# A blockwise triangular inversion that makes one column a step, with an earlier gate and a fifth key buffer

## The chip, the cores and the metric

The program runs on one core of one Trainium2 chip. The metric is the device time of one execution in microseconds (us). Five engines take part, each with its own queue of instructions in order: TensorE (PE; PEld is its weight load), VectorE (DVE), ScalarE (ACT), GpSimd (POOL) and SyncE (SP), which issues the DMAs.

## The reference

A decoder trunk of two layers on a sequence of 1024 with width 1024. Layer 0 mixes by a gated delta rule (GDN) with 8 heads of 128, layer 1 by stick-breaking attention; each is followed by a SwiGLU feed-forward network and a gated embedding. The change touches the GDN alone (and, through the planner's prices, the order elsewhere). Per head and chunk the reference solves a unit lower triangular system:

```python
kk = jnp.einsum('bnhrd,bnhsd->bnhrs', k, k)
a_low = jnp.where(strict, beta[..., None] * kk * decay_mat, 0.0)
rhs = jnp.concatenate([v * beta[..., None], k * (beta * jnp.exp(G))[..., None]], axis=-1)
sol = lax.linalg.triangular_solve(a_low + eye, rhs, left_side=True, lower=True, unit_diagonal=True)
# then, chunk by chunk:
v_new = u_c - jnp.einsum('bhcd,bhde->bhce', w_c, state)
o = jnp.einsum('bhcd,bhde->bhce', q_c, state) + jnp.einsum('bhrs,bhse->bhre', qk_c, v_new)
state = state * gl_c[..., None, None] + jnp.einsum('bhcd,bhce->bhde', k_c, v_new)
```

## The kernel before

The kernel works with chunks of 128 and with sixteen units u = 2h + half (head h, half of the sequence; four chunks each). Projections and the feed-forward network are matmuls of 512 columns, each value split in a high and a low part, so that one product is three matmuls. The small products of the GDN (128 x 128) are in float32 and show as two records each, transposes as one.

**The order is written by a planner at build time.** Every piece of work is a Python generator; `Flow.run` (line 228) steps a simulated clock, which is PE's, and always lets the ready generator of lowest key run; when none is ready it takes the next dense matmul (`gdn_dense`, line 780) as filler. `Flow.cost` (line 114) prices each instruction; on DVE it is 0.069 us plus elements/960. The order in which instructions are emitted is the order of each engine's queue on the chip, so a wrong price doesn't change the result, but puts a PE instruction ahead of its operand.

**GDN.** Dense order (`gdn_order`, line 868): for each head h the keys k of head h+1 (both halves), gates g of h, then q and v of h+1. `gdn_features` (line 885) filters each projection (three DVE steps on `ca`) and puts it through Silu on ACT. `gdn_inv(h)` (line 948) waits at line 954, loads the decay rows (`Gb`: DMA, a mask on POOL, Exp on ACT), transposes the keys into `kt`, makes the triangle `LT`, and takes its four 32 x 32 diagonal blocks through DRAM (`Ld`) into `Ls`, with one partition per eighth part of a block. There the inverse of all blocks of a head is built in `xr` by 31 steps of two DVE instructions each, with `yr` between them (lines 1028 to 1032). The result goes back by DRAM (`Xd`) into `X0`, three rounds of 128 x 128 products join the blocks (`Z`), and the recurrence `gdn_rec(u)` (line 1111) uses it: per chunk a chain PE `rc`, DVE `vin`, PE `r`, DVE `vE`, PE `rc`, DVE `Sm`. `gdn_prep(u)` (line 1069) marks ("p", u) after its `rq`; `cdone` counts finished recurrences. Inversion and recurrence have the same key, ahead of all else. The attention of layer 1 uses two POOL masks per diagonal block (`select`, line 1918).

The loop of the inversion, before:

```python
for t in range(B - 1, 0, -1):
    y = self.g("yr", (P, CG, B))
    nc.vector.tensor_tensor(y[:, :, :t], x[:, :, t : t + 1].to_broadcast([P, CG, t]), Lv[:, :t, t].unsqueeze(1).to_broadcast([P, CG, t]), op=ALU.mult)
    yield
    nc.vector.tensor_tensor(x[:, :, :t], x[:, :, :t], y[:, :, :t], op=ALU.subtract)
```

Of the kernel before, what the change touches and what calls it, by code (L numbers as in the profile page):

```python
# [8 lines left out]
F32 = mybir.dt.float32  # L9
F32R = mybir.dt.float32r  # L10
AF = mybir.ActivationFunctionType
ALU = mybir.AluOpType
# [3 lines left out]
P = 128  # L16
# [3 lines left out]
H = 8  # L20
HW = 512
NC = S // P
# [9 lines left out]
B = 32  # L32
NB = P // B
CG = 8
# [3 lines left out]
def const_table():  # L38

    i = np.arange(P)  # L40
    r, c = i[:, None], i[None, :]
    tab = [b.astype(np.float32) for b in (r == c, r <= c, r >= 0 * c, r >= c, r < c)]
    tab.append(-(r // B > c // B).astype(np.float32))
    g = i[:, None, None] % (B // CG)
    e = np.arange(B)[None, None, :] == CG * g + np.arange(CG)[None, :, None]
    tab += list(e.reshape(P, 2, P).astype(np.float32).transpose(1, 0, 2))
    return np.ascontiguousarray(np.stack(tab, 1))
# [35 lines left out]
class Flow:  # L83
# [29 lines left out]

    def cost(self, eng, op, out, ins, kw):
        n = 1
        for d in out.shape[1:]:
            n *= d
        psum = any(x.space == PSUM for x in ins)
        if eng == "pe":
            if op != "transpose" and ins[0].dtype == F32R:  # L120
                return max(n, P) / 2400.0 + 0.0127
            return max(n, P) * (2 if op == "transpose" else 4) / 2400.0 + (0.003 if op == "transpose" else 0.0107)
        if eng == "dve":
            if op == "memset":
                return 0.06 + n / 3840.0
            tail = 0.06 if any(x.shape[-1] == 1 for x in ins) and n > 1 else 0.0
            fast = op in ("tensor_copy", "tensor_scalar") and not psum
            return 0.069 + tail + n / (1920.0 if fast else 960.0)
        if eng == "act":
            us = (0.052 if psum else 0.094) + n / 1200.0  # L130
            return us + 0.093 * (len(ins) - 1) + (0.235 if "accum_out" in kw else 0.0)
        if op == "tensor_tensor":
            return 0.295 + 0.166 * n if kw.get("op") == ALU.pow else 0.148 + n * 0.002104
        return 0.12 + n / 1085.0

    def shared(self, eng, op, outs, ins, kw, t, c):

# [132 lines left out]
class Net:  # L270
# [366 lines left out]
        flow.mark(("pp", layer))  # L637


    BUFS = {"kf": 5, "qf": 4, "vf": 2, "sg": 2, "Gb": 4, "eGb": 1, "kt": 4, "LT": 2, "vt": 3, "QK": 3, "zz": 2, "Z": 3, "ou": 2, "xe": 2, "ca": 2, "Ls": 1, "xr": 1, "rq": 3, "sc": 2, "yr": 1, "vin": 1}  # L640

    def g(self, tag, shape=(P, HW), dt=F32):
        return self.t(self.gs, tag, shape, dt, bufs=self.BUFS.get(tag, 2))
# [76 lines left out]
    def gdn_gates(self, abs_):  # L720

        nc, gc, ad = self.nc, self.gc, self.ad
        NJ = H * NC
        pt = yield from self.bank()
        ptv = pt[:, : NC * 16].rearrange("p (c j) -> p c j", j=16)
        for c in range(NC):
            nc.tensor.transpose(ptv[:, c], abs_[c // 4][:, (c % 4) * P : (c % 4 + 1) * P], self.ident[:16, :16])
        yield
        t = gc.tile([P, NC, 16], F32, name="abt")
        nc.vector.tensor_copy(t, ptv)  # L730
        self.unbank(pt)
        x = gc.tile([P, H, NC], F32, name="xg")
        tv = t.rearrange("p c j -> p j c")
        nc.vector.tensor_tensor(x, tv[:, :H], ad[:, 1].unsqueeze(2).to_broadcast([P, H, NC]), op=ALU.add)
        yield
        e = gc.tile([P, H, NC], F32, name="eg0")
        nc.scalar.activation(e, x, AF.Abs)
        nc.scalar.activation(e, e, AF.Exp, scale=-1.0)
        ea = gc.tile([P, H], F32, name="ea")
        nc.scalar.activation(ea, ad[:, 0], AF.Exp)  # L740
        nc.scalar.activation(e, e, AF.Ln, bias=1.0)
        yield
        nc.vector.scalar_tensor_tensor(e, x, 0.0, e, op0=ALU.max, op1=ALU.add)
        g = gc.tile([P, H, NC], F32, name="g")
        nc.vector.scalar_tensor_tensor(g, e, -1.0, ea.unsqueeze(2).to_broadcast([P, H, NC]), op0=ALU.mult, op1=ALU.mult)
        yield
        gf = g.rearrange("p h c -> p (h c)")
        pr = yield from self.bank()
        self.mmul(pr[:NJ, :P], gf, self.cst[:, C_TRI])
        yield  # L750
        rows = gc.tile([NJ, 2, P], F32, name="rows")
        nc.vector.tensor_copy(rows[:, 0], pr[:NJ, :P])
        self.unbank(pr)
        yield
        nc.sync.dma_start(self.gD[0], rows[:, 0])
        self.flow.mark("rows")
        nc.scalar.activation(rows[:, 1], rows[:, 0], AF.Exp)
        pG = yield from self.bank()
        self.mmul(pG[:, :NJ], self.cst[:, C_TRI], gf)
        self.mmul(pG[:, NJ : 2 * NJ], self.ones, gf)  # L760
        yield
        nc.sync.dma_start(self.gD[1], rows[:, 1])
        GG = gc.tile([P, 3, NJ], F32, name="GG")
        nc.vector.tensor_copy(GG[:, :2].rearrange("p a j -> p (a j)"), pG[:, : 2 * NJ])
        self.unbank(pG)
        self.neG = gc.tile([P, NJ], F32, name="neG")
        self.nG = gc.tile([P, NJ], F32, name="nG")
        nc.vector.tensor_scalar(self.nG, GG[:, 0], -1.0, None, op0=ALU.mult)
        nc.vector.tensor_tensor(GG[:, 2], GG[:, 1], GG[:, 0], op=ALU.subtract)
        yield  # L770
        EE = gc.tile([P, 3, NJ], F32, name="EE")
        nc.scalar.activation(EE, GG, AF.Exp)
        self.beta = gc.tile([P, H, NC], F32, name="beta")
        nc.scalar.activation(self.beta, tv[:, H:], AF.Sigmoid)
        self.eG, self.gl, self.E = EE[:, 0], EE[:, 1], EE[:, 2]
        yield
        nc.vector.tensor_scalar(self.neG, self.eG, -1.0, None, op0=ALU.mult)
        self.flow.mark("gates")
# [106 lines left out]
    def gdn_features(self, n, u, ps):  # L885

        nc = self.nc
        h, hf = u // 2, u % 2
        yield
        if n == "g":  # L890
            f = self.g("sg")
            nc.scalar.activation(f, ps, AF.Silu)
            self.give("mm")
            self.st[u]["g"] = f
            self.flow.mark(("g", u))
            return
        yield from self.take("xe")
        yield from self.take("ca")
        xe = self.g("xe", (P, HW + 3))
        nc.scalar.copy(xe[:, 3:], ps)  # L900
        self.give("mm")
        if hf == 0:
            nc.gpsimd.memset(xe[:, :3], 0.0)
        else:
            nc.vector.tensor_copy(xe[:, :3], self.conv_tail[n])
        yield
        if hf == 0:
            self.conv_tail[n] = self.g("cy" + n, (P, 3))
            nc.vector.tensor_copy(self.conv_tail[n], xe[:, HW:])
        ca = self.tmp()  # L910
        tl = "qkv".index(n) * H + h
        nc.scalar.activation(ca, xe[:, :HW], AF.Copy, scale=self.conv[:, 0, tl : tl + 1])
        yield
        for j in range(1, 4):
            nc.vector.scalar_tensor_tensor(ca, xe[:, j : j + HW], self.conv[:, j, tl : tl + 1], ca, op0=ALU.mult, op1=ALU.add)
            yield
        f = self.g(n + "f")
        nc.scalar.activation(f, ca, AF.Silu)
        self.give("xe", "ca")
        self.st[u][n] = f  # L920
        self.flow.mark((n, u))
# [26 lines left out]
    def gdn_inv(self, h):  # L948

        nc, flow = self.nc, self.flow  # L950
        us = (2 * h, 2 * h + 1)
        chunks = [slice(c * P, (c + 1) * P) for c in range(4)]
        j0 = us[0] * 4
        yield lambda: flow.done("rows") and self.cdone >= us[0] - 2 and (h == 0 or ("p", us[0] - 1) in flow.at) and (h < 2 or ("w", us[0] - 3) in flow.at)
        Gb = [self.g("Gb") for _ in us]

        def decay():
# [16 lines left out]
        for i, u in enumerate(us):  # L974
# [3 lines left out]
            kt = self.g("kt")  # L978
# [12 lines left out]
        yield lambda: flow.done("gates")  # L991
        bt = self.beta.rearrange("p h c -> p (h c)")[:, j0 : j0 + 8]
        nc.vector.tensor_tensor(rkb, rk, bt, op=ALU.mult)
        nc.vector.tensor_tensor(brk2, rkb, rk, op=ALU.mult)
        yield lambda: flow.done(("D", h))
        LT = self.g("LT", (P, 2, HW))
        for i, u in enumerate(us):
# [23 lines left out]
        Ls = self.g("Ls", (P, B * B))  # L1021
        src = Ld.rearrange("c b s r -> (c b) (s r)").unsqueeze(1).to_broadcast([8 * NB, B // CG, B * B])
        nc.sync.dma_start(Ls, src)
        x = self.g("xr", (P, CG, B))
        nc.scalar.copy(x, self.masks[:, 1:].rearrange("p a (j s) -> p (a j) s", s=B))
        yield
        Lv = Ls.rearrange("p (s r) -> p s r", r=B)
        for t in range(B - 1, 0, -1):
            y = self.g("yr", (P, CG, B))
            nc.vector.tensor_tensor(y[:, :, :t], x[:, :, t : t + 1].to_broadcast([P, CG, t]), Lv[:, :t, t].unsqueeze(1).to_broadcast([P, CG, t]), op=ALU.mult)  # L1030
            yield
            nc.vector.tensor_tensor(x[:, :, :t], x[:, :, :t], y[:, :, :t], op=ALU.subtract)
            yield
        flow.mark(("x", h))
        nc.sync.dma_start(Xd.rearrange("c b r k -> (c b r k)").rearrange("(p n) -> p n", p=P), x.rearrange("p j s -> p (j s)"))
# [1087 lines left out]
```

## Time and profile before

| what | value |
|---|---|
| median of 3 runs | 2801.99 us (2799.51 to 2804.23) |
| the profiled execution | 2799.09 us |
| its span, first to last instruction | 2797.3 us |
| mean granted TensorE clock | 0.997 |
| busy: PE, PEld, DVE, ACT, POOL | 98%, 81%, 70%, 47%, 31% |

The GDN fills the first 660 us of the span or so, the attention about 1500 to 1950. A PE that is busy is not a PE at its peak, because a matmul's record is longer than the time until the next one starts; so the number of matmuls in a stretch says more than the busy share. All instructions bear line 64 (a helper that records them); they are told apart by their tiles. In the rows, `tp<-cst,kf` reads "into tile tp, from cst and kf".

### The profile page before, as it was taken

The page shows a single profiled execution, that of the slowest core. Times are in us where ns is not written, and L with a number is a line of the kernel's source. Part 1 is how long each engine was busy: PE and PEld are TensorE (multiplying, and loading weights), DVE is VectorE, ACT ScalarE, POOL GpSimd, SP SyncE. Part 2 cuts the span into 40 slices and gives each one's busy share as a digit, 9 for nine tenths or more (in the row PEclk, how much of TensorE's full clock was granted, in tenths as well). Part 3 has the DMA queues.
Part 4 walks back from the last instruction along what each step waited for, and adds up shares of the span by engine and source line. Part 5 has one row for each costly group of instructions (what it writes and reads, how often), then busy time and mean ns, then how long its engine had stood idle before and what let it go on. Part 6 is the DMA issues. An engine that isn't in the chain of part 4 may idle for free.

```text
span 2797.3 us, 37777 instructions
## 1 busy us (share of the span) xinstructions
PE 2750.1 (98%) x13203; PEld 2271.7 (81%) x13203; DVE 1969.8 (70%) x3733; ACT 1326.0 (47%) x2694; POOL 870.4 (31%) x742
## 2 busy tenths in 40 slices
PE   9999999999999999999999999999999999999999
PEld 7888888878878888888878888887878888888777
DVE  7778877884776565477867778787696565557783
ACT  6655555543443343322335778787543433322241
POOL 0111111100166666443201222221036766734400
PEclk9999999999999999999999999999999999999999
DMA  4412222237524444587333111114524444477622
GB/s 146 143 58 81 67 74 74 74 111 252 178 91 158 154 147 147 211 314 307 138 132 102 50 53 57 54 57 153 207 70 151 145 154 148 157 287 283 273 98 105
DMA packets 165631, 395.89 MB, mean 142 GB/s; under 512 B 34048, under 2 KB 35392, under 8 KB 155968
## 3 DMA queue, kind: packets, MB, share of 16 engines
q1 hardware_dynamic: 165440, 393.48, 39.7%
q8 instruction: 104, 1.70, 0.3%
q14 instruction: 87, 0.71, 0.1%
HBM read 274.29 MB, written 119.11 MB: 141 GB/s over the span
## 4 chain that ended last, share of the span: by engine, by line
PE 79%; DVE 12%; ACT 3%; DMA 3%; issue 3%; SPq 1%; POOL 1%; ACTq 0%; DVEq 0%; POOLq 0%
PE dn L64 38%; PE mm L64 29%; PE tp L64 3%; PE z L64 3%; PE c L64 2%; PE o L64 2%; DVE x L64 1%; DVE yr L64 1%; DVE ca L64 1%; DVE xr L64 1%; PE po L64 1%; DVE wlo L64 1%; DVE u L64 1%; DVE v L64 1%; SPq L64 1%
## 5 line engine op out<-in xcount | busy, mean ns | idle before, releaser
L64 PE MATMUL mm<-x,whi 128*128 128x512 f32 x2848 | 941.0, 400 | 8.5 <-DVE x L64 5.4
L64 PEld LDWEIGHTS mm<-x,whi 128*128 128x128 f32 x2848 | 529.6, 189 | 107.9 <-DVE x L64 8.4
L64 PE MATMUL mm<-x,wlo 128*128 128x512 f32 x1424 | 569.3, 400 | 0.0
L64 PE MATMUL dn<-x,whi 128*128 128x512 f32 x1776 | 548.9, 390 | 1.8 <-DVE v L64 0.9
L64 POOL TENSOR_TENSOR wlo<-raw,whi 128x512 fp32r<-128x512 f32 x236 | 345.5, 1485 | 441.1 <-ACT whi L64 414.8
L64 ACT CAST whi<-raw 128x1024 fp32r<-128x1024 f32 x231 | 242.9, 1052 | 447.7 <-DVE raw L64 262.5
L64 PEld LDWEIGHTS dn<-x,whi 128*128 128x128 f32 x1776 | 333.1, 188 | 73.7 <-DVE x L64 2.9
L64 PE MATMUL dn<-x,wlo 128*128 128x512 f32 x888 | 345.7, 389 | 0.0
L64 PEld LDWEIGHTS mm<-x,wlo 128*128 128x128 f32 x1424 | 269.0, 189 | 46.1 <-issue 0.2
L64 PE MATMUL dn<-hx,whi 128*128 128x512 f32 x864 | 266.5, 389 | 0.3 <-DVE hx L64 0.2
L64 DVE TENSOR_TENSOR tt<-u,tt 128x512 fp32r<-128x512 f32 x140 | 143.6, 1026 | 81.8 <-ACT tt L64 81.7
L64 PEld LDWEIGHTS dn<-x,wlo 128*128 128x128 f32 x888 | 166.7, 188 | 34.4
L64 PEld LDWEIGHTS dn<-hx,whi 128*128 128x128 f32 x864 | 162.1, 188 | 34.9 <-DVE hx L64 0.9
L64 DVE TENSOR_TENSOR v<-v,dn 128x512 f32<-128x512 f32 x112 | 76.6, 685 | 156.3 <-PE dn L64 155.8
L64 DVE TENSOR_TENSOR wlo<-raw,whi 128x512 fp32r<-128x512 f32 x226 | 154.4, 696 | 29.4 <-ACT whi L64 29.1
L64 PE MATMUL dn<-hx,wlo 128*128 128x512 f32 x432 | 168.5, 390 | 3.4 <-POOL wlo L64 3.4
L64 POOL TENSOR_TENSOR wlo<-sw,whi 128x512 fp32r<-128x512 f32 x102 | 144.3, 1432 | 2.0 <-ACT whi L64 2.0
L64 ACT CAST tt<-u 128x512 fp32r<-128x512 f32 x140 | 84.9, 620 | 123.7 <-DMA yD<-tt 100.3
L64 DVE TENSOR_TENSOR E<-E,dn 128x512 f32<-128x512 f32 x132 | 90.0, 684 | 69.9 <-PE dn L64 67.7
L64 DVE SCALAR_TENSOR_TENSOR ca<-xe,conv,ca 128x512 f32<-128x512 f32 x144 | 108.4, 754 | 8.9 <-ACT ca L64 8.5
L64 POOL TENSOR_TENSOR rs<-ms,nhalf 128x4 f32<-128x4 f32 x11 | 12.4, 1123 | 328.9 <-DVE ms L64 328.9
L64 PE MATMUL dn<-y,whi 128*128 128x512 f32 x352 | 108.3, 389 | 0.0
(379 smaller groups left out, 5159.5 us busy)
## 6 DMA issues: line engine op xcount, KB each, us to landing
yD<-tt SPq DMA_DIRECT2D x296, 256.0 KB, 2.2
x<-yD SPq DMA_DIRECT2D x58, 1024.0 KB, 11.7
raw<-f_s SPq DMA_DIRECT2D x84, 512.0 KB, 3.6
raw<-d_s SPq DMA_DIRECT2D x40, 512.0 KB, 4.0
raw<-w_in SPq DMA_DIRECT2D x33, 512.0 KB, 3.6
hx<-yD SPq DMA_DIRECT2D x16, 1024.0 KB, 11.2
x<-oD SPq DMA_DIRECT2D x27, 512.0 KB, 6.7
raw<-g_out SPq DMA_DIRECT2D x16, 512.0 KB, 5.8
```

Of the source, the lines that this page charges most:

```text
L64: r = issue(*args, **kw)
```

## The change

The inverse is built the other way round. Before, step t took column t of the block, multiplied it with column t of the triangle (elements 32 apart in `Ls`) and subtracted the outer product from all columns to its left. After, step s makes column s alone: the columns to its right are multiplied with row s of the triangle (elements side by side), and a `tensor_reduce` sums each row of products into column s. The last columns and the unit entries are put in beforehand by two ACT copies instead of one. The sign moves into `LT` (`brk2` gets a factor of -1), so the mask of the joining step turns positive.

Further: `kt` gets five buffers, `sc` three; the gate at line 954 opens one recurrence earlier; small tiles of `gdn_gates` move into `vt` buffers; the filter's tail is kept per head. The planner's prices change: `tensor_reduce` is priced by its input, a DVE input with stepped elements costs 0.085 us more, a POOL mask 0.4 us plus elements/1400.

```diff
-    tab.append(-(r // B > c // B).astype(np.float32))
+    tab.append((r // B > c // B).astype(np.float32))
...
-        for d in out.shape[1:]:
+        for d in (ins[0] if op == "tensor_reduce" else out).shape[1:]:
...
+            if any(x.shape[-1] > 1 and x.ap[-1][0] > 1 for x in ins):
+                tail += 0.085
...
-        return 0.12 + n / 1085.0
+        return 0.4 + n / 1400.0 if op == "affine_select" else 0.1 + n / 1085.0
...
-    BUFS = {... "kt": 4, ... "sc": 2, ...}
+    BUFS = {... "kt": 5, ... "sc": 3, ...}
...
-        t = gc.tile([P, NC, 16], F32, name="abt")
+        room = self.g("vt")
+        t = room[:, : NC * 16].rearrange("p (c j) -> p c j", j=16)
...
-        yield lambda: flow.done("rows") and self.cdone >= us[0] - 2 and (h == 0 or ("p", us[0] - 1) in flow.at) and (h < 2 or ("w", us[0] - 3) in flow.at)
+        yield lambda: flow.done("rows") and self.cdone >= us[0] - 3 and (h < 2 or ("p", us[0] - 3) in flow.at) and (h < 2 or ("w", us[0] - 3) in flow.at)
...
-        nc.vector.tensor_tensor(brk2, rkb, rk, op=ALU.mult)
+        nc.vector.scalar_tensor_tensor(brk2, rkb, -1.0, rk, op0=ALU.mult, op1=ALU.mult)
...
         x = self.g("xr", (P, CG, B))
-        nc.scalar.copy(x, self.masks[:, 1:].rearrange("p a (j s) -> p (a j) s", s=B))
+        y = self.g("yr", (P, CG, B))
+        rows = self.masks[:, 1:].rearrange("p a (j s) -> p (a j) s", s=B)
+        nc.scalar.copy(x[:, :, B - 1], rows[:, :, B - 1])
+        nc.scalar.copy(y[:, :, : B - 1], rows[:, :, : B - 1])
         yield
         Lv = Ls.rearrange("p (s r) -> p s r", r=B)
-        for t in range(B - 1, 0, -1):
-            y = self.g("yr", (P, CG, B))
-            nc.vector.tensor_tensor(y[:, :, :t], x[:, :, t : t + 1].to_broadcast([P, CG, t]), Lv[:, :t, t].unsqueeze(1).to_broadcast([P, CG, t]), op=ALU.mult)
-            yield
-            nc.vector.tensor_tensor(x[:, :, :t], x[:, :, :t], y[:, :, :t], op=ALU.subtract)
+        for s in range(B - 2, -1, -1):
+            nc.vector.tensor_tensor(y[:, :, s + 1 :], x[:, :, s + 1 :], Lv[:, s, s + 1 :].unsqueeze(1).to_broadcast([P, CG, B - 1 - s]), op=ALU.mult)
+            yield
+            nc.vector.tensor_reduce(x[:, :, s], y[:, :, s:], axis=mybir.AxisListType.X, op=ALU.add)
             yield
```

## Rows read from the trace of the kernel before

**Rows 1.** The page: its first line, and section 1 (busy time by engine).

```profile
span 2797.3 us, 37777 instructions
PE 2750.1 (98%) x13203; PEld 2271.7 (81%) x13203; DVE 1969.8 (70%) x3733; ACT 1326.0 (47%) x2694; POOL 870.4 (31%) x742
```

**Rows 2.** Windows: length, busy by engine, clock, DMA; feed-forward, then attention.

```profile
1050.00:1100.00 50.00, 50.00 (x222) 41.40 (x221) 29.19 (x39) 18.92 (x27) 32.23 (x23) 1.00 0.47 159
...
1600.00:1650.00 50.00, 50.00 (x251) 41.88 (x250) 40.53 (x85) 40.76 (x97) 9.28 (x18) 1.00 0.14 48
```

**Rows 3.** Chain of waits, one run of 128 x 128 products: start, length, what.

```profile
275.88 2.68 PE tp L64 x24
```

**Rows 4.** Windows, columns as above: GDN from 167.6; inversion 5; between; inversion 6.

```profile
167.60:610.90 443.30, 435.27 (x2497) 360.31 (x2494) 355.00 (x1018) 247.28 (x717) 51.57 (x63) 1.00 0.24 74
429.30:472.10 42.80, 42.23 (x224) 33.73 (x225) 41.12 (x127) 23.19 (x73) 3.73 (x5) 1.00 0.15 50
472.10:500.50 28.40, 27.92 (x180) 24.59 (x178) 15.70 (x39) 16.20 (x42) 4.47 (x5) 1.00 0.35 107
500.50:543.30 42.80, 42.34 (x225) 33.68 (x225) 41.13 (x127) 23.18 (x72) 3.73 (x5) 1.00 0.14 50
```

**Rows 5.** The same windows, instructions of tile mm alone (matmuls of 512 columns).

```profile
167.60:610.90 443.30, 327.21 (x1178) 208.27 (x1178) 0.00 (x0) 29.40 (x50) 1.00 0.24 74
429.30:472.10 42.80, 35.12 (x126) 22.19 (x127) 0.00 (x0) 2.92 (x5) 1.00 0.15 50
472.10:500.50 28.40, 18.61 (x68) 11.72 (x66) 0.00 (x0) 1.76 (x3) 1.00 0.35 107
500.50:543.30 42.80, 35.26 (x127) 22.16 (x127) 0.00 (x0) 2.92 (x5) 1.00 0.14 50
```

**Rows 6.** Weight loads' waits, 50 to 660 us: total us, times, longest.

```profile
PEld r L64 <- DVE vin L64: 10.9, 29, 1.1
PEld rc L64 <- DVE vE L64: 10.5, 36, 0.6
PEld rc L64 <- DVE Sm L64: 7.1, 20, 1.2
```

**Rows 7.** Groups on DVE, 90 to 615 us: count, busy us, mean ns, idle before.

```profile
L64 DVE TENSOR_TENSOR yr<-xr,Ls 128x248 f32<-128x248 f32 (+30 forms) x248 | 97.4, 393 | 12.0 <-DMA Ls<-Ld 7.9
...
L64 DVE TENSOR_TENSOR xr<-xr,yr 128x248 f32<-128x248 f32 (+30 forms) x248 | 72.9, 294 | 4.1
```

**Rows 8.** Groups by shape on DVE, 0 to 640 us, columns as in 7.

```profile
L64 DVE TENSOR_TENSOR yr<-xr,Ls 128x248 f32<-128x248 f32 x8 | 4.8, 601 | 7.9 <-DMA Ls<-Ld 7.9
...
L64 DVE TENSOR_TENSOR xr<-xr,yr 128x248 f32<-128x248 f32 x8 | 3.3, 412 | 0.1
...
L64 DVE CAST x<-vf 128x512 fp32r<-128x512 f32 x4 | 1.7, 421 | 0.0
...
L64 DVE TENSOR_TENSOR xr<-xr,yr 128x8 f32<-128x8 f32 x8 | 1.4, 172 | 0.1
```

**Rows 9.** Group on ACT, 0 to 650 us: the reading of a folded sum.

```profile
L64 ACT ACTIVATION_READ_ACCUMULATOR junk<-tp 128x1 f32 x128 | 25.1, 196 | 0.0
```

**Rows 10.** PE's waits over the whole span: total us, times, longest.

```profile
PE tp L64 <- DMA X<-Xd: 3.8, 4, 2.7
```

**Rows 11.** Timeline around the gate of head 6: start, length, engine, operation.

```profile
472.24 1.01 POOL L64 TENSOR_TENSOR rq<-mq,nhalf 128x4 f32<-128x4 f32 x1 [5.83 <-DVE xe L64]
476.56 1.78 POOL L64 TENSOR_SCALAR_AFFINE_SELECT Gb<-Gb 128x512 f32<-128x512 f32 x2 [3.32 <-DMA Gb<-gD]
```

**Rows 12.** The same stretch on DVE.

```profile
474.79 0.75 DVE L64 SCALAR_TENSOR_TENSOR ca<-xe,conv,ca 128x512 f32<-128x512 f32 x1
...
476.06 1.78 DVE L64 SCALAR_TENSOR_TENSOR ca<-xe,conv,ca 128x512 f32<-128x512 f32 x2
```

**Rows 13.** The same stretch on ACT.

```profile
481.75 0.63 ACT L64 ACTIVATE kf<-ca 128x512 f32<-128x512 f32 x1
...
494.52 0.40 ACT L64 COPY xr<-masks 128x256 f32<-128x256 f32 x1
```

More of the change, by code (lines that the diff above doesn't have):

```diff
@@ L637, in ple_products @@
         flow.mark(("pp", layer))
-    BUFS = {"kf": 5, "qf": 4, "vf": 2, "sg": 2, "Gb": 4, "eGb": 1, "kt": 4, "LT": 2, "vt": 3, "QK": 3, "zz": 2, "Z": 3, "ou": 2, "xe": 2, "ca": 2, "Ls": 1, "xr": 1, "rq": 3, "sc": 2, "yr": 1, "vin": 1}
+    BUFS = {"kf": 5, "qf": 4, "vf": 2, "sg": 2, "Gb": 4, "eGb": 1, "kt": 5, "LT": 2, "vt": 3, "QK": 3, "zz": 2, "Z": 3, "ou": 2, "xe": 2, "ca": 2, "Ls": 1, "xr": 1, "rq": 3, "sc": 3, "yr": 1, "vin": 1}
     def g(self, tag, shape=(P, HW), dt=F32):
@@ L728, in gdn_gates @@
         yield
-        t = gc.tile([P, NC, 16], F32, name="abt")
+        room = self.g("vt")
+        t = room[:, : NC * 16].rearrange("p (c j) -> p c j", j=16)
         nc.vector.tensor_copy(t, ptv)
         self.unbank(pt)
-        x = gc.tile([P, H, NC], F32, name="xg")
+        x, e, g = (room[:, (2 + i) * NJ : (3 + i) * NJ].rearrange("p (h c) -> p h c", c=NC) for i in range(3))
         tv = t.rearrange("p c j -> p j c")
@@ L735, in gdn_gates @@
         yield
-        e = gc.tile([P, H, NC], F32, name="eg0")
         nc.scalar.activation(e, x, AF.Abs)
@@ L743, in gdn_gates @@
         nc.vector.scalar_tensor_tensor(e, x, 0.0, e, op0=ALU.max, op1=ALU.add)
-        g = gc.tile([P, H, NC], F32, name="g")
         nc.vector.scalar_tensor_tensor(g, e, -1.0, ea.unsqueeze(2).to_broadcast([P, H, NC]), op0=ALU.mult, op1=ALU.mult)
         yield
-        gf = g.rearrange("p h c -> p (h c)")
+        gf = room[:, 4 * NJ : 5 * NJ]
         pr = yield from self.bank()
@@ L750, in gdn_gates @@
         yield
-        rows = gc.tile([NJ, 2, P], F32, name="rows")
+        more = self.g("vt")
+        rows = more[:NJ, : 2 * P].rearrange("p (a c) -> p a c", c=P)
         nc.vector.tensor_copy(rows[:, 0], pr[:NJ, :P])
@@ L762, in gdn_gates @@
         nc.sync.dma_start(self.gD[1], rows[:, 1])
-        GG = gc.tile([P, 3, NJ], F32, name="GG")
+        GG = more[:, 2 * P : 2 * P + 3 * NJ].rearrange("p (a j) -> p a j", j=NJ)
         nc.vector.tensor_copy(GG[:, :2].rearrange("p a j -> p (a j)"), pG[:, : 2 * NJ])
@@ L904, in gdn_features @@
         else:
-            nc.vector.tensor_copy(xe[:, :3], self.conv_tail[n])
+            if (n, h) not in self.conv_tail:
+                yield lambda: (n, h) in self.conv_tail
+            nc.vector.tensor_copy(xe[:, :3], self.conv_tail[n, h])
         yield
         if hf == 0:
-            self.conv_tail[n] = self.g("cy" + n, (P, 3))
-            nc.vector.tensor_copy(self.conv_tail[n], xe[:, HW:])
+            self.conv_tail[n, h] = self.g("cy" + n, (P, 3))
+            nc.vector.tensor_copy(self.conv_tail[n, h], xe[:, HW:])
         ca = self.tmp()
```

## The prediction

> **What bounds the kernel now.** I read the page first: PE is busy for 98% of the span, no other engine for more than 70% [rows 1]. The change takes nothing from PE, so all it can win is time in which PE works below its rate. The busy share hides this time, since records overlap; I therefore count matmuls. In the feed-forward stretch, where every matmul has 512 columns, 222 of them take 50 us, 0.2252 us each [rows 2]. A run of 24 records of 128 x 128 takes 2.68 us, 0.1117 each [rows 3]. These are PE's rates.
>
> Now the GDN, from 167.6 to 610.9 us (six inversions). It has 2497 matmuls [rows 4], 1178 of them with 512 columns [rows 5]. At PE's rates these need 1178 x 0.2252 + 1319 x 0.1117 = 265.3 + 147.3 = 412.6 us; the stretch takes 443.3. So 30.7 us are stalls, though the same row calls PE busy for 435.27. The next windows tell where they lie. While head 5 is inverted (429.3 to 472.1): 126 x 0.2252 + 98 x 0.1117 = 39.3 of 42.8 us, a stall of 3.5. While head 6 is inverted: 127 and 98, 39.5 of 42.8, 3.3. Between the two: 68 and 112, 27.8 of 28.4, 0.6 [rows 4, 5]. PE loses its time while DVE works off an inversion. There DVE is busy for 41.12 of 42.8 us, 96%, and between for 15.70 of 28.4, 55% [rows 4].
>
> Who is late, the waits say: the weight loads of the recurrence's products wait for DVE's `vin`, `vE` and `Sm`, 10.9 + 10.5 + 7.1 = 28.5 us [rows 6]. Part of this is covered by the matmuls before, so it is a ceiling, but it names the chain: recurrence steps queued on DVE among the steps of an inversion.
>
> Why the planner didn't leave room shows in its price. It gives both steps of the inversion 0.069 us + elements/960. The rows give 393 ns for the mean product (`yr`) and 294 for the mean subtraction (`xr`) at the same sizes [rows 7]. At 248 elements the gap is 601 to 412 [rows 8]: it grows with the elements. The product is the one that reads `Ls` in steps of 32 elements. So each inversion runs 31 x 0.099 = 3.1 us behind the plan by its products alone, about what PE stalls in each of the two windows (3.3 and 3.5, less some 0.9 that a stretch of this length loses without an inversion too: 0.6 x 42.8/28.4).
>
> **The change part by part.**
>
> The product. 248 of them keep their sizes and now read `Ls` along a row. I take the subtraction's 294 ns, the nearest row: two tensors from the same memory, elements side by side. 248 x (393 - 294) = -24.5 us of DVE. If the step is not the reason, it is 0.
>
> The reduction takes the subtraction's place, 248 times. It reads 8 x (32 - s) elements, 4216 a head, where the subtraction took 3968. By the slope of the subtraction, (412 - 172)/240 = 1.0 ns an element [rows 8], that is +0.25 us a head, +2.0 in all. The trace holds no reduction on DVE. Bound below: the CAST with one tensor in takes 421 ns for 512 elements [rows 8], about half a nanosecond an element with the small subtraction's 172 taken off; at half the slope 136 elements (the mean reduction) gain some 0.07 us, -17 us in all. Bound above: each also pays for reading out its sum as ACT does, 196 ns [rows 9]: +49. I take +2.0, because what it reads is nearest to the subtraction.
>
> The Trainium skill ("VectorE: DVE Perf Modes", section "Rules for kernel authors") speaks against putting `tensor_reduce` on a hot path: it calls it the slowest DVE operation and always of single rate. By the single rate of that page the lower bound of -17 falls away and the +2.0 stays; the row of the subtraction already runs near one element per nanosecond. No run so far shows a reduction.
>
> Net on DVE: -24.5 + 2.0 = -22.5 us, 2.8 an inversion. Chain and count of instructions stay: 62 dependent steps with a yield between.
>
> What of it reaches PE? The six inversions of the stretch have a lag of 6 x 3.1 = 18.6 us by their products, beside stalls of 30.7, of which 9.4 are the base (0.6 in every 28.4 us) and 21.3 are beyond it; so up to all of DVE's saving can come back. Bounds 0 and 22.5. I take 0.6 of it, since the order is planned anew and other work stays in DVE's queue: 22.5 x 0.6 = -13.5 us.
>
> The landing of `X`. PE waits 3.8 us for it, 2.7 of them once [rows 10]. An inversion that ends up to 2.8 us earlier against a plan that stays takes most of that: -2.
>
> The gate and the fifth `kt`. For head 6 the old gate opens after `rq` at 472.24 + 1.01 [rows 11]. The inversion needs both keys of its head, and the second one is put through Silu at 481.75 [rows 13]: it comes in the dense order, which PE sets. So the gate isn't what comes last, and a wider gate brings the triangle little; I take 0. What it moves is all the work behind it that needs no key: two `Gb` DMAs on SP, the POOL mask of two instructions, 1.78 us [rows 11], and Exp on ACT. They can now fall into the inversion before, where DVE is full. While the mask ran, two filter steps took 1.78 us [rows 12], where one alone takes 0.75, so at least 0.28 us were lost. Bounds per head: 0 and 1.78 (DVE stands for the whole mask); times six heads 0 to 10.7; I take 0.28, +1.7. On SP they pass the weight loads, which PE isn't seen waiting for; on POOL the small powers of the recurrence's output, 1.01 us each [rows 11].
>
> The ACT copies: one of 0.40 us [rows 13] becomes two, of 8 and of 248 elements; 0 to 0.4 us more per head. Cover: the copy ends at 494.92, and the first product of head 6 starts about 500, when `Ls` has landed; without cover 3 us in all. The factor in `brk2`, the sign of the mask, the third `sc`, the tiles moved to `vt` and the kept filter tails add no instruction: 0.
>
> The planner's new prices reorder other stages too. In the attention PE is busy for all of a 50 us window [rows 2], so there is little to win and as little to repair; I take 0 and allow 3 us either way.
>
> Sum: -13.5 - 2 + 1.7 = -13.8, say -14. The profiled execution took 2799.09 us, 1.79 more than its span; with the change it would take 2785. The median of the runs is 2.9 above it, 2801.99, so I predict 2788.
>
> **The rivals.**
>
> A, no change: DVE's queue stays full because the inversion is greedy. It has first claim; if its steps are shorter, the planner puts the next ones in earlier, and the recurrence finds as many ahead of it as before. Against: what is late in the rows is a delay against the plan, and shorter steps end sooner either way. For: 96% busy leaves little room [rows 4]. Time: the -2 and the +1.7 remain, 2802.
>
> B, slower: the reduction is dear. Place: DVE within the eight inversions. Price: +196 ns each by the bound above, so DVE gets +49 - 24.5 + 2 = +26 us, and at 0.6 PE loses 16: 2818. It decides from a mean reduction of 294 + 99 = 393 ns, where the saving is used up; slower by more than 0.2% (5.6 us) takes 5.6/0.6/248 = 0.038 us more, some 430 ns. For: nothing in the trace bounds it better. Against: it reads one tensor, side by side.
>
> C, slower: the mask and the Exp that the gate moves hold the full DVE for their whole length, 10.7 us, while the saving reaches PE by a quarter only: -5.6 + 10.7 = +5, with the reorder's 3 about 2809.
>
> D, the change does more: the whole lag and the landing waits vanish. 22.5 + 3.8 = 26: 2776.
>
> E, the change doesn't do what it says: the stepped read isn't what costs, products stay at 393 ns and DVE is +2. Then 2802 + 2 x 0.6 + 1.7, about 2805, counted with A.
>
> **How the numbers follow.** The forecast (2788, from 2780 to 2796) has a chance of 0.54, D 0.10, A with E 0.20, B 0.09, C 0.07. Measured beside no change, about 0.2% (5.6 us) can be told apart. So faster 0.64, same 0.20, slower 0.16. The range runs from 2773 (D with the reorder's 3 us) to 2808, up to C, leaving out B and tails of C and D, under 2 in 10.
>
> **What would show it.** The mean product falls to about 294 ns; the mean reduction lies near 300. In the windows of an inversion, counts at PE's rates leave 1.5 to 2 us of stall in place of 3.4; the waits of `r` and `rc` for DVE fall from 28.5 us to about half. Keys still come when they did relative to the triangle. Wrong would be: a reduction beyond 400 ns (B); shorter steps with the same waits (A); mask and Exp inside an inversion with longer DVE steps beside them (C); a gain that lies outside the GDN.

## The result and the profile after

| | before | after |
|---|---|---|
| median | 2803.11 us (4 runs, 2799.51 to 2805.97) | 2787.12 us (4 runs, 2784.26 to 2788.42) |
| profiled execution | 2799.09 us | 2787.44 us |

The ratio is 0.9946, with a 95% interval of 0.9933 to 0.9958: 16 us less, between 12 and 19. The prediction was 2788. One execution below, the profiled one of j_rec_first_old_gate, took 3898.98 us at a granted clock of 0.654; its median leaves it out and its waits aren't given.

PE has the same number of matmuls as in [rows 1] and a shorter span. From the page after:

```profile
span 2785.7 us, 37779 instructions
PE 2741.7 (98%) x13203; PEld 2278.1 (82%) x13203; DVE 1951.7 (70%) x3733; ACT 1324.3 (48%) x2701; POOL 860.4 (31%) x742
```

The next two views answer to [rows 4] and [rows 5]: windows from the end of the second inversion (head 1) to the end of the last, then inversion 5, the time between, and inversion 6. First all instructions, then those of tile mm.

```profile
169.50:596.10 426.60, 423.45 (x2494) 360.24 (x2493) 341.30 (x1015) 245.53 (x724) 48.78 (x60) 1.00 0.24 75
418.90:457.50 38.60, 38.12 (x205) 31.86 (x205) 36.65 (x117) 25.95 (x71) 5.81 (x8) 1.00 0.20 68
457.50:489.00 31.50, 31.34 (x207) 27.45 (x206) 18.99 (x50) 14.62 (x47) 2.64 (x2) 1.00 0.27 81
489.00:527.10 38.10, 37.57 (x199) 31.08 (x199) 36.43 (x114) 24.69 (x68) 3.52 (x7) 1.00 0.28 91
```

```profile
169.50:596.10 426.60, 321.93 (x1160) 205.17 (x1159) 0.00 (x0) 28.79 (x49) 1.00 0.24 75
418.90:457.50 38.60, 34.25 (x127) 22.38 (x127) 0.00 (x0) 3.48 (x6) 1.00 0.20 68
457.50:489.00 31.50, 20.22 (x69) 11.74 (x67) 0.00 (x0) 1.78 (x3) 1.00 0.27 81
489.00:527.10 38.10, 33.85 (x127) 22.37 (x127) 0.00 (x0) 2.54 (x5) 1.00 0.28 91
```

The same count as in the prediction: 1160 x 0.2252 + 1334 x 0.1117 = 410.2 us of work in 426.6, so 16.4 us of stalls where there were 30.7. Inversion 5: 127 and 78 matmuls, 37.3 of 38.6 us, a stall of 1.3 (before 3.5). Inversion 6: 127 and 72, 36.6 of 38.1, 1.5 (before 3.3). Between: 69 and 138, 30.9 of 31.5, 0.6, as before. So the stalls of this stretch fell by 14.3 us. Counted in the same way inside all six inversions of it, they fell from 19.9 to 8.5 us: 11.4 of the 14.3 lie inside inversions.

The spans of the two profiled executions differ by 11.6, so 2.7 us were given back in other stretches. TensorE's clock can account for that. Around the end of the attention its mean was 0.97 of full speed before and 0.95 after (windows of 130 us, before and then after; the clock is the last number but two):

```profile
1940.00:2070.00 130.00, 126.18 (x558) 102.44 (x557) 95.88 (x169) 65.72 (x104) 11.50 (x16) 0.97 0.47 160
1925.00:2055.00 130.00, 126.83 (x554) 104.51 (x553) 95.19 (x169) 66.86 (x106) 11.71 (x17) 0.95 0.46 160
```

Summed over the clock records of the traces from the end of the GDN on, stretches at 0.50 (1.2 GHz in place of 2.4) cost 6.4 us before and 12.3 after. Whether that comes with the new order or by chance of these two executions isn't shown. The medians differ by 16.0, more than the two spans.

The waits of the weight loads, 50 to 645 us, which the last recurrence lies within (total us, times, longest), answer to [rows 6]:

```profile
PEld r L64 <- DVE vin L64: 5.3, 19, 0.9
PEld rc L64 <- DVE vE L64: 4.4, 21, 0.5
...
PEld rc L64 <- DVE Sm L64: 1.8, 8, 0.5
```

11.5 us, where there were 28.5. The groups of the inversion on DVE, 90 to 600 us (count, busy us, mean ns, idle before), answer to [rows 7]:

```profile
L64 DVE TENSOR_REDUCE xr<-yr 128x8 f32<-128x16 f32 (+30 forms) x248 | 72.7, 293 | 5.2
L64 DVE TENSOR_TENSOR yr<-xr,Ls 128x8 f32<-128x8 f32 (+30 forms) x248 | 72.6, 293 | 11.8 <-DMA Ls<-Ld 7.6
```

and by shape, as in [rows 8]:

```profile
L64 DVE TENSOR_REDUCE xr<-yr 128x8 f32<-128x256 f32 x8 | 3.3, 417 | 0.1
L64 DVE TENSOR_TENSOR yr<-xr,Ls 128x248 f32<-128x248 f32 x8 | 3.3, 412 | 0.1
...
L64 DVE TENSOR_REDUCE xr<-yr 128x8 f32<-128x16 f32 x8 | 1.4, 169 | 0.6
```

The product at 248 elements fell from 601 to 412 ns, exactly the subtraction's time of before. The reduction takes 417 ns for 256 elements: it costs by what it reads, like an operation of two tensors.

### The profile page after: what moved, and what is told of

The parts are those of the page before. It is cut to its first block, busy times and chain, and to the rows that moved or that the text cites. A ratio compares the mean times of both kernels' runs of the same rounds, so it can differ in the third digit from the quotient of the medians.

```text
span 2785.7 us, 37779 instructions
## 1 busy us (share of the span) xinstructions
PE 2741.7 (98%) x13203; PEld 2278.1 (82%) x13203; DVE 1951.7 (70%) x3733; ACT 1324.3 (48%) x2701; POOL 860.4 (31%) x742
## 4 chain that ended last, share of the span: by engine, by line
PE 86%; DVE 7%; ACT 4%; issue 2%; DMA 1%; POOL 1%; ACTq 0%; POOLq 0%
PE dn L64 38%; PE mm L64 34%; PE tp L64 4%; PE z L64 3%; PE c L64 2%; PE o L64 2%; DVE x L64 1%; PE po L64 1%; PE rc L64 1%; PE r L64 1%; DVE u L64 1%; ACT junk L64 1%; ACT L64 1%; DVE v L64 1%; PE st L64 1%
## 5 line engine op out<-in xcount | busy, mean ns | idle before, releaser
L64 POOL TENSOR_TENSOR rs<-ms,nhalf 128x4 f32<-128x4 f32 x11 | 12.3, 1122 | 330.7 <-DVE ms L64 330.7
```

The lines of the kernel that those rows point to most:

```text
L64: r = issue(*args, **kw)
```

## The experiments

Three theories were put up. **1, lag:** PE stalls because the chip runs behind the plan, and the stepped product is what the plan prices too low. **2, load:** PE stalls because DVE has too much to do during an inversion, whatever the plan knows. **3, gate:** the gain comes from the wider gate. The times, each with the ratio to runs of before on the same chip, and the sum of the three waits of r and rc for DVE, 50 to 680 us (before 28.5, after 11.5). They ran on three chips, so the ratios are what can be compared. The small moves (tiles of `gdn_gates`, filter tails) stay in all kernels but l_rank_before:

| label | what | median us | ratio (95%) | waits us |
|---|---|---|---|---|
| c_loop | new loop alone | 2787.89 | 0.9943 (0.9931 to 0.9956) | 12.6 |
| a_old_gate | all but the gate | 2785.40 | 0.9933 (0.9920 to 0.9946) | 13.4 |
| g_no_mask_price | all but the POOL prices | 2785.91 | 0.9939 (0.9926 to 0.9951) | 10.9 |
| i_gate_only | gate alone | 2811.53 | 1.0025 (1.0016 to 1.0034) | 31.5 |
| k_step_price | step's price alone | 2795.38 | 0.9973 (0.9964 to 0.9982) | 23.2 |
| b_prices | all new prices alone | 2805.88 | 1.0006 (0.9997 to 1.0015) | 18.2 |
| d_underpriced | fast product, plan lags | 2799.03 | 0.9986 (0.9978 to 0.9995) | 18.9 |
| e_column_known | slow product, plan knows | 2797.99 | 0.9986 (0.9977 to 0.9995) | 18.1 |
| f_column_unknown | slow product, plan lags | 2810.79 | 1.0032 (1.0019 to 1.0045) | 20.4 |
| l_rank_before | before, recurrence first | 2800.16 | 0.9993 (0.9985 to 1.0002) | 24.9 |
| h_rec_first | after, recurrence first | 2780.94 | 0.9923 (0.9910 to 0.9937) | 12.7 |
| j_rec_first_old_gate | h with the old gate | 2784.62 | 0.9937 (0.9923 to 0.9950) | no profile |

**Which part brings the gain.** The loop alone, on the old gate and the old prices. The edit is the changed kernel with

```diff
-    BUFS = {... "kt": 5, ... "sc": 3, ...}
+    BUFS = {... "kt": 4, ... "sc": 2, ...}
-            if any(x.shape[-1] > 1 and x.ap[-1][0] > 1 for x in ins):
-                tail += 0.085
-        return 0.4 + n / 1400.0 if op == "affine_select" else 0.1 + n / 1085.0
+        return 0.12 + n / 1085.0
-        ... self.cdone >= us[0] - 3 and (h < 2 or ("p", us[0] - 3) in flow.at) ...
+        ... self.cdone >= us[0] - 2 and (h == 0 or ("p", us[0] - 1) in flow.at) ...
```

> Only the new loop (row products, reduction, the sign) with the small tiles moved; old gate, four kt, two sc, old planner prices. Theory 1 (PE stalls by the lag of the chip behind the plan, which the stepped product causes): the product now runs near its price, so nearly the whole gain stands without the rest, 2786 to 2791. Theory 2 (PE stalls because DVE has too much work in an inversion): the same, 2786 to 2791. Theory 3 (the wider gate brings the gain): about 2800 to 2804.

Measured 2787.89: the loop, with the small moves, is the whole gain, and theory 3 falls. The counterpart puts the old gate and buffers alone back (first and last pair of lines of that diff):

> All of the change but the wider gate, with four kt and two sc. Theories 1 and 2: 2785 to 2790, as the whole change. Theory 3: about 2797 to 2803.

Measured 2785.40. Without the gate the kernel is no slower; whether it is faster can't be told, the intervals overlap. The gate without the loop (old loop, old prices, new gate with its buffers):

> Only the wider gate with five kt and three sc; old loop, old prices. Theories 1 and 2: the second key of a head, not the gate, is what the triangle waits for, so 2800 to 2806. Theory 3: 2788 to 2795.

Measured 2811.53, outside of what any theory said: on the old loop the gate with its buffers costs 8 us (4 to 10 by the interval). Its waits, weight loads 50 to 680 us, and PE's own near 104 us:

```profile
PEld r L64 <- DVE vin L64: 14.7, 33, 1.7
PEld rc L64 <- DVE vE L64: 9.4, 37, 0.8
PEld rc L64 <- DVE Sm L64: 7.4, 22, 1.1
```

```profile
104.60 0.79 PE L64 MATMUL r<-Z,whi 128*128 128x512 f32 x1 [3.97 <-ACT sg L64]
```

The waits rise from 28.5 to 31.5, and a new one of 4 us comes in while head 1 is prepared: a product into a bank that ACT has yet to empty. ACT's copy out of that bank waits in its turn, for a DMA that writes `sg` out:

```profile
103.96 0.59 ACT L64 COPY sg<-r 128x512 f32<-128x512 f32 x1 [3.29 <-DMA ppD<-sg]
```

In the changed kernel the same wait is there, and one more, in PE's waits over the whole span:

```profile
PE r L64 <- ACT sg L64: 3.5, 1, 3.5
...
PE mm L64 <- ACT ca L64: 1.8, 1, 1.8
```

c_loop and a_old_gate, with the old gate, don't have the first one. Gate and buffers were only moved together, so which of them brings it isn't shown. The POOL price was undone by itself as well (the two `return` lines of the diff):

> The changed kernel with the old price of the POOL mask (and of the other POOL work). The mask's price takes no part in the gain: 2784 to 2791. If it were a main part: 2795 or more.

Measured 2785.91: on the new loop it takes no part.

**Lag or load.** On the old loop, the step's price alone lets the plan know the slow product; DVE's work stays.

> Old loop, old gate, and of the new planner prices only the step's 0.085 us; the mask keeps its old price. If the 16 us that the old loop lost at other places under both new prices come by the mask's price, this one shows the gain of a known step: 2790 to 2798. If a plan that knows DVE's load only moves PE's stalls to other steps: 2800 to 2806.

Measured 2795.38, 8 us less than before with the same work on DVE. That is lag, and about half of the gain. Its profiled execution took 2803.34, 8 us more than the median: from the end of its second inversion to the end of its last (426.6 us) it has 2406 matmuls, 1129 of them of `mm`, so still 29.7 us of stalls, at a mean clock of 0.99. So the trace doesn't show where the 8 us came from. The same with the POOL prices too:

> Only the new planner prices on the old loop: the stepped product is priced 0.085 us dearer, DVE's work stays as it was. Theory 1: the plan now knows the product, so PE is given its operands later but in step; the stall in the windows of an inversion falls from 3.4 us to about 1.5, time 2788 to 2795. Theory 2: DVE's work is unchanged, so the stalls stay, 2800 to 2805. Theory 3: 2800 to 2805.

Measured 2805.88, no gain, though the waits for DVE fell to 18.2. Beside k_step_price the POOL prices cost 9 us on the old loop (1.0006 to 0.9973). PE's timeline at the worst place, and windows of all engines there (length, busy by engine, granted clock, DMA):

```profile
408.40 1.12 PE L64 MATMUL tp<-cst,kf 128*128 128x128 f32 x4 [4.89 <-ACT kf L64]
```

```profile
403.50:408.40 4.90, 0.01 (x2) 0.00 (x1) 1.12 (x8) 4.68 (x17) 1.01 (x1) 0.81 0.13 38
408.40:412.00 3.60, 3.60 (x13) 2.96 (x14) 0.92 (x2) 3.50 (x15) 0.39 (x1) 0.50 0.18 29
412.00:416.00 4.00, 4.00 (x29) 3.66 (x28) 1.91 (x6) 1.21 (x3) 1.29 (x2) 0.83 0.35 131
```

and ACT before it (start, length, operation):

```profile
399.13 1.28 ACT L64 ACT_TABLE_LOAD   x1
400.42 2.46 ACT L64 ACTIVATE Gb<-Gb,nG 128x128 f32<-128x128 f32 x8
...
406.42 1.28 ACT L64 ACT_TABLE_LOAD   x1
407.72 0.63 ACT L64 ACTIVATE kf<-ca 128x512 f32<-128x512 f32 x1
```

The place of the transposition in PE's queue says that in the plan the key was there by about 403.5. On the chip ACT was busy with the table load and the Exp of the decay until 402.9, and then with sums of squares, a copy and the second table load: 4.68 us of work in the 4.9 that PE waited. Behind the wait the clock stood at 0.50 for 3.6 us and at a mean of 0.83 over the next 4.0: 0.50 x 3.6 + 0.17 x 4.0 = 2.5 us that the wait cost on top. One new order thus hit a place where the plan is late for another reason. Why ACT was so far behind its plan there wasn't tried.

To part lag from load under one gate and one set of other prices, three kernels were made from the changed one. d lowers the price of the row product alone, so that the plan lags as before and DVE's work stays small:

```diff
+            if op == "tensor_tensor" and out.name.startswith("yr"):
+                return 0.069 + n / 960.0 - n * 0.00079
```

> The changed kernel, but its planner prices the row product 0.79 ns an element too low, as much as the stepped product was underpriced before: the chip's work is the new one, the plan lags again by 3 us an inversion. Theory 1 (lag): the stalls come back, 2797 to 2803, and the waits of r and rc for DVE rise to 20 us or more. Theory 2 (DVE's load): 2785 to 2790, waits as in the changed kernel.

Measured 2799.03, as theory 1 has it, and the waits rise to 18.9, a little short of the 20. The product and the reduction on DVE are those of the changed kernel:

```profile
L64 DVE TENSOR_REDUCE xr<-yr 128x8 f32<-128x16 f32 (+30 forms) x248 | 73.0, 294 | 5.6
L64 DVE TENSOR_TENSOR yr<-xr,Ls 128x8 f32<-128x8 f32 (+30 forms) x248 | 72.0, 290 | 14.5 <-DMA Ls<-Ld 5.8 <-ACT sg L64 4.3
```

So a wrong price alone, with nothing slower on the chip, costs 12 us. e makes the product slow and tells the plan:

```diff
-            nc.vector.tensor_tensor(..., Lv[:, s, s + 1 :].unsqueeze(1) ...)
+            nc.vector.tensor_tensor(..., Lv[:, s + 1 :, s].unsqueeze(1) ...)
```

> The changed kernel, but the product reads a column of the triangle in place of the row, so that its step is 32 elements again (the inverse is left wrong by that). The plan knows it (0.085 us). DVE's work is that of before, the lag is not. Product 390 ns in the mean. Theory 1: 2787 to 2793. Theory 2: 2797 to 2804.

Measured 2797.99, as theory 2 has it: 11 us more than the changed kernel, with a product of 394 ns again:

```profile
L64 DVE TENSOR_TENSOR yr<-xr,Ls 128x8 f32<-128x8 f32 (+30 forms) x248 | 97.8, 394 | 10.5 <-ACT vt L64 3.4 <-DMA Ls<-Ld 2.7
```

This also settles that the step is what makes the product slow: the same engine, sizes and order, another stride. f takes the price away as well (e without the 0.085):

> As the run before, with the column in place of the row, but without the price for the step: load and lag are both those of before. Theory 1 and theory 2 both: 2797 to 2805. If this comes out below 2793, neither the load nor the lag is the reason, and what is left is the gate and the mask's price.

Measured 2810.79, above all that was expected, 24 us over the changed kernel and 8 over the kernel before, which has the same load and lag. The wide gate, which costs as much in i_gate_only, is the likely reason. The four kernels make a square: lag alone +12, load alone +11, both +24. Neither theory holds alone. On the old gate the same comparison is c_loop (neither), k_step_price (load alone) and before (both): 0.9943, 0.9973 and 1, so +8 and +16 us.

That lag and load simply add up is less firm. Windows of d, e and f from the end of the second inversion to the end of the last, first all instructions, then those of tile mm:

```profile
167.00:608.90 441.90, 435.61 (x2528) 365.01 (x2528) 344.30 (x1023) 254.27 (x744) 47.58 (x64) 1.00 0.23 74
191.20:611.70 420.50, 410.12 (x2388) 344.87 (x2388) 346.76 (x987) 232.34 (x682) 48.20 (x59) 1.00 0.23 73
173.10:617.10 444.00, 432.01 (x2496) 359.21 (x2494) 358.73 (x1016) 245.00 (x719) 50.49 (x60) 1.00 0.23 73
```

```profile
167.00:608.90 441.90, 330.22 (x1190) 211.93 (x1191) 0.00 (x0) 29.34 (x50) 1.00 0.23 74
191.20:611.70 420.50, 306.22 (x1108) 196.62 (x1108) 0.00 (x0) 27.61 (x47) 1.00 0.23 73
173.10:617.10 444.00, 322.17 (x1162) 206.28 (x1162) 0.00 (x0) 29.42 (x50) 1.00 0.23 73
```

At PE's rates the stalls are 24.5, 28.0 and 33.3 us, where the changed kernel has 16.4: +8, +12 and +17. Both kinds show, but their sum is more than what both together cost there; the rest of the times comes from other stretches. One more reservation: e's price is flat, the true surcharge grows with the elements (0.79 ns each), so a part of e's 11 us may still be lag.

**Rank.** Rival A said that the inversion stands ahead of the recurrence in DVE's queue by its rank. The edit, on the changed kernel and on the one before:

```diff
-                flow.spawn(self.gdn_inv(h), 0)
+                flow.spawn(self.gdn_inv(h), 0.5)
```

> The changed kernel, but the inversion ranks behind the recurrence in the planner (0.5 in place of 0). If the recurrence is late because the inversion is emitted ahead of it (rival A of the prediction), 2 to 4 us less than the changed kernel, 2783 to 2785, with fewer waits of r and rc for DVE. If it is late only by lag, 2785 to 2791.

> The kernel before with the inversion ranked behind the recurrence, nothing else. If the recurrence's stalls come by rank, a good part goes without a new loop: 2793 to 2798, r and rc waiting less than 20 us for DVE. If they come by lag and load, 2800 to 2806.

On the changed kernel (h_rec_first) 2780.94, the lowest median of all, 6 us below the changed kernel, with intervals that overlap a little. On the kernel before (l_rank_before) 2800.16, not told apart from no change. With the old gate:

> The changed kernel with the old gate (four kt, two sc) and the inversion ranked behind the recurrence. If the wide gate costs a wait of PE for ACT near 104 us (3.5 us in the changed kernel, absent where the gate is old) and the rank saves some 5 us, both add up: 2776 to 2781. If these differences are only accidents of the order: 2781 to 2788.

Measured 2784.62, the same as a_old_gate without the rank. So rank brought some 6 us in one setting, where the intervals overlap, and nothing that can be told in two. The waits for DVE don't fall in h (12.7, in the changed kernel 11.5), and h's profiled execution took 2787.99, 7 us more than its median, so its profile doesn't show where the 6 us went. This stays open: that h is faster than the changed kernel or a_old_gate isn't shown.

## Why the prediction was right

- **What bounds the kernel.** Counting matmuls at PE's rates gave 30.7 us of stalls, 19.9 of them inside inversions. They fell by 14.3, 11.4 of these inside inversions. The sum was 13.8, the medians differ by 16.0.
- **Product.** Taken at 294 ns, measured 293; -24.8 us in the busy times (97.4 to 72.6). The bound of 0 fell; so did rival E.
- **Reduction.** Taken at +2.0 us; measured -0.2 (72.9 to 72.7). The bounds of -17 and +49 were far off on both sides, rival B fell: 293 ns is well below the 393 from which it would have decided. The Trainium skill ("VectorE: DVE Perf Modes", section "Rules for kernel authors") has it as the slowest DVE operation with a single rate. The single rate agrees with the trace (417 ns for 256 elements read, 412 for a product of 248); slowest it isn't.
- **What of it reaches PE.** The step with the right size and half the reason. The prediction argued from a lag alone, and its 0.6 was chosen with no row behind it; that it came out is partly luck. The square of kernels shows that lag and load each cost 11 to 12 us alone, and the new loop removed both at once. k_step_price shows that the lag alone, with the price put right, is worth about half. The 13.5 was also meant for all eight inversions, while 14.3 us came back in the stretch of six. Ahead of that stretch the waits of 3.5 and 1.8 us that are new stand against 2.7 us that PE no longer waits for X there.
- **The landing of X.** -2 was taken, and the 3.8 us of [rows 10] are gone entirely from PE's waits.
- **The gate.** The forecast had the mask and the Exp falling into a full inversion, and the gain from the gate at 0. The masks of head 6 now run in inversion 5; a product of four elements beside them took 0.55 us, where such a one took 0.16 elsewhere. Timeline, POOL and then DVE, of the kernel after:

```profile
426.99 0.64 POOL L64 TENSOR_SCALAR_AFFINE_SELECT Gb<-Gb 128x512 f32<-128x512 f32 x1
```

```profile
427.08 0.55 DVE L64 TENSOR_TENSOR t<-t,rq 128x4 f32<-128x4 f32 x1
```

  That is 0.4 us at this head, near the 0.28 that was taken. But before, the masks had lengthened DVE's steps too. Beside head 1's mask a subtraction of 168 elements took 0.67 us, where the median is 0.33 (POOL, then DVE, of the kernel before):

```profile
107.91 0.94 POOL L64 TENSOR_SCALAR_AFFINE_SELECT Gb<-Gb 128x512 f32<-128x512 f32 x1 [3.96 <-DMA Gb<-gD]
```

```profile
108.36 0.67 DVE L64 TENSOR_TENSOR xr<-xr,yr 128x168 f32<-128x168 f32 x1
```

  Over all sixteen masks, DVE steps beside them took 3.2 us more than the medians of their shapes before, and 3.0 after. So +1.7 priced a cost that was there already. What the prediction missed is head 1: the wider gate also opens for it earlier, and PE then waits 3.5 us for a bank. On the old loop the gate with its buffers costs 8 us; on the new loop its cost can't be told from nothing (a_old_gate).
- **Rival C** (mask and Exp hold DVE) was right as a place and far too dear. **Rival A** fell as a forecast, since the waits fell by 60% with the rank unchanged; its mechanism isn't settled, since a change of rank brought some 6 us in one setting and nothing in two.
- **Other stages.** Taken as 0, give or take 3; 2.7 us were given back there in the profiled executions, less than the 5.9 that the lower clock cost after the GDN. A cost of the new order isn't shown.

## What to carry to other kernels

When one engine is "98% busy", count its instructions at the rate of an undisturbed stretch and look where the count falls short; the other engine that is full in just those windows is the one to relieve. If the order is fixed ahead by prices, a wrong price can cost as much as slow work, as d and e show: measure each operation with its strides, and correct the price and the operation together. After any change of order look for new single waits, for a good plan can lose its gain at one place, as b_prices did.

## What was not expected of the hardware

- On VectorE an input in float32 read in steps of 32 elements cost 0.79 ns an element more: 601 against 412 ns at 248 elements, and nothing at 8.
- `tensor_reduce` over the innermost dimension, with eight results, cost no more than an elementwise operation on what it reads: 417 ns for 256 elements, 169 for 16.
- After a wait of 4.89 us PE ran at 0.50 of its clock, 1.2 GHz, for 3.6 us and at a mean of 0.83 over the next 4.0: the stall went on costing 2.5 us after it had ended.
